# Foreign rows of the recurrence gates gathered by DMA, 48 of them stacked as high and low parts

## The chip, the cores and the metric

The kernel runs on one core of one Trainium2 chip. The metric is the device time in microseconds of one execution. The time of a kernel is the median over several executions.

## The reference

Two layers over 256 tokens with a width of 1024. Each layer norms x, projects it in one wide product, and feeds two branches. Branch A is an attention with 8 heads whose keys an indexer has chosen. Branch B is a recurrence of width 1408: a causal convolution of four taps, then two gates r and i, a scan over positions, and an output product. Both branches are gated, added, projected and added to x. A last norm ends the computation.

The change touches only the gates of branch B:

```
xb = x.reshape(B, S, RNN_BLOCKS, RNN_BLOCK_DIM)       # 16 blocks of 88 channels
r = sigmoid(einsum('bsnc,ncd->bsnd', xb, w_r) + b_r)  # each block has its own 88x88 matrix
i = sigmoid(einsum('bsnc,ncd->bsnd', xb, w_i) + b_i)
```

A gate channel depends on the 88 convolved channels of its own block alone. All products keep nearly the precision of float32.

## The kernel before

**Layout.** Channels lie on partitions, tokens along the free dimension. The 1408 channels of branch B are 11 tiles of 128 (`KR`). Blocks of 88 do not line up with tiles of 128, so the blocks that a tile of outputs touches reach into one or both neighbour tiles. These rows of a neighbour are called foreign here. The block matrices are laid out on the host as one block-diagonal 1408x1408 matrix, and a gate multiplies 128x128 cuts of it.

**Precision.** Every operand is split into a high part (rounded to the matmul's type, `copy`) and a low part (the rest, `sub`). A product takes three matmuls, high weight by high data, low weight by high data and high weight by low data (`mm3`, L617); the matmuls are recorded under L493, the line of the helper `mm`. A data tile `xs` is `[128, 2, 256]`: high and low halves of 256 tokens.

**Gates.** `gate_parts` (L96) lists what a gate of tile j multiplies. Odd tiles below 10 have foreign rows on both sides that fit in half a tile each; for these `gr` (L944) copies half of a neighbour's `xs` into a shared tile `xm` (two copies for each mixed tile, 10 in a layer), and the gate multiplies the tile itself and `xm`. The other tiles multiply whole neighbour tiles, whose weights are mostly zeros. Tiles 2, 4, 6 and 8 need three tiles, all others two. Each of the two gates r and i needs three matmuls of 256 columns for each tile: 12 in a gate with two tiles, 18 in one with three, 156 in a layer.

**The weight stream.** All weights are cut on the host into 128x128 blocks in the order in which the plan uses them (`weight_stream`, L1188; `unit_blocks`, L108) and loaded as chunks of 8 blocks, 512 KB, by SP's DMA queue (SPq). A chunk lands in one of 4 `raw` buffers (`RAWS`), ScalarE or VectorE rounds it to `wh`, VectorE subtracts to get `wl`; both have 6 buffers (`WBUF`). All DMAs of the kernel are issued by SP.

**Order.** `plan` (L62) writes out the units of a layer: the indexer; then for j = 0..10 the recurrence input `xr` and its gate `gr` (24 matmuls each) with light units of other projections between them, and `gate` of tile j-3 behind `gr` of tile j (`DELAY`); after the last `gr` the gates of tiles 8, 9 and 10, each behind two light units; then attention and the outputs. Every operation is first entered in a list. `Program.issue` (L266) then simulates the engines with costs written in the code and fixes the order of instructions on each engine, SP's DMAs included; the engines carry it out in that order and wait on semaphores for their data. TensorE's order follows the position in the plan. An operation that makes a new tile needs a free buffer of its pool: `r2` has 38 (`xs`, `xm` and others), `f1` has 21 of 1 KB per partition (convolution outputs `xc`, gate `sg`, `y`, `asq`, scan results `hh`, and others). `choose` (L375) lets an operation take a buffer ahead of earlier ones only while enough stay free for those (up to 5 in `f1`, `KEEP`, L406). After gates 2, 5, 8 and 10 a `tail` of three (at last two) tiles runs the exponentials, the scan into `hh` and the products.

Of the kernel before, what the change touches and what calls it, by code (L numbers as in the profile page):

```python
# [11 lines left out]
F32 = mybir.dt.float32  # L12
F32R = mybir.dt.float32r
# [4 lines left out]
P = 128  # L18
D = 1024
T = 256  # L20
# [3 lines left out]
KR = NR // P  # L24
NH = 8
NB = 16
BD = NR // NB
# [19 lines left out]
NPAR = _c  # L47


def gate_rows(j):  # L50

    lo = (P * j) // BD * BD
    hi = ((P * j + P - 1) // BD + 1) * BD
    return list(range(lo // P, (hi - 1) // P + 1))


DELAY = 3
# [38 lines left out]
def gate_parts(j):  # L96


    rows = gate_rows(j)
    if len(rows) == 3:  # L100
        first = (P * j) // BD * BD
        last = ((P * j + P - 1) // BD + 1) * BD
        if P * j - first <= 64 and last - P * (j + 1) <= 64:
            return [j, (j + 1, j - 1)]
    return rows


def unit_blocks(u):  # L108

    n = u[0]  # L110
    if n == "ik":
        return [("in80", k, OFF["ik"]) for k in range(KD)]
    if n == "attn":
        return []
    if n in ("iq", "ga", "xr", "gr", "q", "k"):
        return [("in", k, OFF[n] + u[1] * P) for k in range(KD)]
    if n == "gate":
        return [(w, i, u[1] * P) for w in ("rg", "ig") for i in gate_parts(u[1])]
    if n in ("v", "mb", "ma"):
        return [("in", 2 * u[2] + k, OFF[n] + u[1] * 512 + a * P) for k in range(2) for a in range(4)]  # L120
    if n == "yb":
        return [("or", k, u[1] * 512 + a * P) for k in range(KR) for a in range(4)]
    if n == "ya":
        return [("oa", k, u[1] * 512 + a * P) for k in range(KD) for a in range(4)]
    return [("o", k, u[1] * P) for k in range(u[2], u[3])]
# [64 lines left out]
def real(a):  # L190
    return a.ap() if isinstance(a, V) else a
# [222 lines left out]
def trunk(ctx, tc, xT, pos, par, wst, out):  # L414
    nc = tc.nc
# [3 lines left out]
    fp = ctx.enter_context(tc.tile_pool(name="fp", bufs=1))  # L419
    pp = ctx.enter_context(tc.tile_pool(name="pp", bufs=1, space=bass.MemoryType.PSUM))  # L420
    ctx.enter_context(tc.manual_schedule())
    pg = Program()
    cnt = [0]

    def nm(s):
        cnt[0] += 1
        return f"{s}{cnt[0]}"


    def const(s, shape, dt=F32, bufs=1, tag=None):  # L430
        return pg.tile(cp, tag or s, [P] + shape, dt, nm(s), bufs)

    def r2(s):
        return pg.tile(rp, "r2", [P, 2, T], F32R, nm(s), R2)
# [7 lines left out]
    def f1(s):  # L442
        return pg.tile(fp, "f1", [P, T], F32, nm(s), F1)

# [4 lines left out]
    def act(o, i, func, **kw):  # L449
        c = (50 if i.psum() else 94) + 0.833 * o.size() + (200 if "accum_out" in kw else 0)  # L450
        aps = [kw[k] for k in ("scale", "bias") if isinstance(kw.get(k), V)]
        outs = [o] + ([kw["accum_out"]] if "accum_out" in kw else [])
        pg.op("act", c + 93 * len(aps), outs, [i] + aps,
              lambda: nc.scalar.activation(real(o), real(i), func, **{k: real(v) for k, v in kw.items()}),
              TABS.get(func))

    def copy(o, i):

        n = o.size()
        pg.op("act", (50 if i.psum() else 94) + 0.833 * n, [o], [i],  # L460
              lambda: nc.scalar.activation(real(o), real(i), AF.Copy),  # L461
              alt=(67 + 1.046 * n if i.psum() else 69 + 0.52 * n,
                   lambda: nc.vector.tensor_copy(real(o), real(i))))
# [5 lines left out]
    def mul(o, a, b):  # L469
        tt(OP.mult, o, a, b)  # L470
# [20 lines left out]
    def mm(o, w, m, start, stop, grp=False, cost=None):  # L491
        pg.op("pe", cost or (m.size() + 32) / 2.4, [o], [w, m],
              lambda: nc.tensor.matmul(real(o), real(w), real(m), start=start, stop=stop, skip_group_check=grp))  # L493
# [14 lines left out]
    class Stream:  # L508
        def __init__(self):
            self.pos = 0  # L510
            self.raws = {}
            self.parts = {}
            self.nload = 0
# [65 lines left out]
    ws = Stream()  # L579
# [4 lines left out]
    first = ws.load(QUARTERS)  # L584
# [13 lines left out]
    def pc(n, i=0):  # L598
        return prm[:, PC[n] + i:PC[n] + i + 1]
# [17 lines left out]
    def mm3(o, rhs, first, last, grp=False):  # L617
        wh, wl = ws.block()
        mm(o, wh, rhs[0], first, False, grp)
        mm(o, wl, rhs[0], False, False, grp)  # L620
        mm(o, wh, rhs[1], False, last, grp)

    def proj(o, rhs):
        n = len(rhs)
        for k in range(n):
            mm3(o, rhs[k], k == 0, k == n - 1)

    def split(dst, src):

        copy(dst[0], src)  # L630
        sub(dst[1], src, dst[0].bitcast(F32))

    def halves(t):
        return t[:, 0, :], t[:, 1, :]
# [148 lines left out]
    class Layer:  # L783
        def __init__(self, l, xg, norm):
            self.l = l
            self.xg = xg
            self.norm = norm
            self.h = []
            self.sga, self.sma, self.smb = {}, {}, {}
            self.xc, self.xs, self.rix, self.sy, self.g = {}, {}, {}, {}, {}  # L790
            self.rope = {}
            self.mix = {}
            self.aT = []
            self.m = []
            self.banks = {}
            self.wk = [const("wk0", [P]), const("wk1", [T])]
            self.kh = const("kh", [T], F32R)
            self.kl = const("kl", [T], F32R)
            self.iwq = const("iwq", [2, 16])
# [144 lines left out]
        def gr(self, j):  # L944
            ps = self.banks["rnn"]
            proj(ps[:, 1, :], self.h)
            n = KR * self.l + j
            c = f1("xc")
            w = [pc("cw", 4 * n + i) for i in range(4)]
            act(c, ps[:, 0, :], AF.Identity, scale=w[3], bias=pc("cb", n))  # L950
            for i in (2, 1, 0):
                s = 3 - i
                stt(c[:, s:], ps[:, 0, :T - s], w[i], c[:, s:], OP.mult, OP.add)
            t = r2("xs")
            split(halves(t), c)
            self.xc[j], self.xs[j] = c, halves(t)
            for i, h in ((j - 1, slice(0, 64)), (j + 1, slice(64, 128))):
                if 0 <= i < KR and any(isinstance(r, tuple) for r in gate_parts(i)):
                    if i not in self.mix:
                        self.mix[i] = r2("xm")  # L960
                        self.xs[i + 1, i - 1] = halves(self.mix[i])
                    copy(self.mix[i][h], t.bitcast(F32)[h])
            u = f1("sg")
            act(u, ps[:, 1, :], AF.Sigmoid)
            mul(u, u, ps[:, 1, :])
            self.sy[j] = u

        def gate(self, j):
            rows = gate_parts(j)
            ps = bank("pq", "gps")  # L970
            for gi in range(2):
                for n, i in enumerate(rows):
                    mm3(ps[:, gi, :], self.xs[i], n == 0, n == len(rows) - 1)
            n = KR * self.l + j
            t = r2f("rix")
            r, ix, y = t[:, 0, :], t[:, 1, :], f1("y")
            act(r, ps[:, 0, :], AF.Sigmoid, bias=pc("br", n))
            act(ix, ps[:, 1, :], AF.Sigmoid, bias=pc("bi", n))
            mul(ix, ix, self.xc[j])
            act(y, r, AF.Tanh, scale=cpos[:, n:n + 1])  # L980
            self.rix[j] = (t, y)
            if j in GROUPS:
                self.tail(GROUPS[j])
# [175 lines left out]
    n = 0  # L1159
    for w in (1, 2, 2, 2, 1):  # L1160
        o = f2("fo")[:, :w, :]
# [10 lines left out]
QUARTERS = 2  # L1172
R2 = 38
F2 = 5
F1 = 21
RAWS = 4
WBUF = 6
LEAD = 2000.0
# [9 lines left out]
def weight_stream(w_in, w_rg, w_ig, w_oa, w_or, w_o):  # L1188

    out = []  # L1190
    for l in range(L):
        mats = {"in": w_in[l], "or": w_or[l], "oa": w_oa[l], "o": w_o[l]}
        mats["in80"] = w_in[l].copy()
        mats["in80"][:, OFF["ik"] + 80:] = 0
        for n, w in (("rg", w_rg[l]), ("ig", w_ig[l])):
            d = np.zeros((NR, NR), w.dtype)
            for b in range(NB):
                d[b * BD:b * BD + BD, b * BD:b * BD + BD] = w[b]
            mats[n] = d
        for u in plan():  # L1200
            for n, r, c in unit_blocks(u):
                if isinstance(r, tuple):
                    lo, up = r[0] * P, r[1] * P + 64
                    out.append(np.concatenate([mats[n][lo:lo + 64, c:c + P], mats[n][up:up + 64, c:c + P]]))
                else:
                    out.append(mats[n][r * P:r * P + P, c:c + P])
    assert len(out) == NBLK
    out += [np.zeros((P, P), w_in.dtype)] * (NCH * 8 - NBLK)
    a = np.stack(out).reshape(NCH, 8, P, P)
    return np.ascontiguousarray(a.transpose(0, 2, 1, 3)).reshape(NCH, P, 1024)  # L1210
# [45 lines left out]
```

## Time and profile before

| | |
|---|---|
| median of 3 executions | 716.36 us (716.25, 716.36, 757.32) |
| the profiled execution | 716.78 us, of which the span is 715.0 us |
| TensorE matmuls (PE) | 699.0 us busy, 4880 of them |
| VectorE (DVE) | 599.8 us busy |
| ScalarE (ACT) | 499.2 us busy |
| GpSimd (POOL) | 7.7 us busy |
| DMA, queue of SP | 120.44 MB, 51.3% of 16 engines' span |
| granted TensorE clock | 0.995 of 2.4 GHz |

PE rows are matmuls, PEld rows are weight loads, which overlap them. A matmul's recorded duration (283 ns) overlaps with that of the next, so the pace of a run of matmuls is read from the length of the run divided by its count. SPq rows are DMAs as SP issues them. `L493` is the one line that records nearly every matmul, so matmuls are told apart by the names of their tiles: `rps` (xr and gr), `gps` (the gates), `ga`, `ma`, `mb` (light units), `yb`, `ya`, `ops` (outputs).

### The profile page before, as it was taken

To read this page: it belongs to the slowest core of one execution; us is meant where nothing else is said; L and a number is where in the kernel's file an instruction comes from. 1 tells how busy PE (TensorE), PEld (TensorE's weight loads), DVE (VectorE), ACT (ScalarE), POOL (GpSimd) and SP (SyncE) were. 2 spreads that over 40 slices of the span, in tenths; PEclk is the share of its full clock that TensorE was granted. 3 is DMA by queue.
4 is the path that set the end of the run, shared out by engine and by line. 5 is a ranking of instruction groups with operands and counts; after the bars stand their busy time and mean duration, and the time that the engine had idled before them with its cause. 6 is when DMAs were issued, how large, how long until landed. Compare 5 with 4: busy or idle time off the path is not lost.

```text
span 715.0 us, 12814 instructions
## 1 busy us (share of the span) xinstructions
PE 699.0 (98%) x4880; PEld 652.5 (91%) x4880; DVE 599.8 (84%) x1181; ACT 499.2 (70%) x811; POOL 7.7 (1%) x18
## 2 busy tenths in 40 slices
PE   7999999999999999999999999999999999999996
PEld 6998999999999998888999899999999898988895
DVE  6989999899798959857779998989889886896652
ACT  7997685899895648434669776698879674764432
POOL 0000000000000000000000000010000000000000
PEclk9999999999999999999999999999999999999998
DMA  7646455555656452655553554555555545445501
GB/s 255 207 160 215 159 171 181 179 177 189 198 173 207 148 179 86 203 180 178 177 177 116 182 175 166 184 182 181 179 202 180 199 152 177 148 130 180 191 1 60
DMA packets 35485, 121.26 MB, mean 170 GB/s; under 512 B 3936, under 2 KB 6496, under 8 KB 35424
## 3 DMA queue, kind: packets, MB, share of 16 engines
q1 hardware_dynamic: 35424, 120.44, 51.3%
q8 instruction: 38, 0.62, 0.3%
q14 instruction: 23, 0.19, 0.1%
HBM read 119.38 MB, written 1.05 MB: 168 GB/s over the span
## 4 chain that ended last, share of the span: by engine, by line
PE 86%; ACT 6%; DVE 3%; issue 1%; DMA 1%; SPq 1%; DVEq 0%; ACTq 0%
PE rps L493 16%; PE yb L493 8%; PE ops L493 7%; PE k L493 6%; PE q L493 6%; PE ma L493 6%; PE v L493 6%; PE ya L493 6%; PE gps L493 5%; PE ga L493 5%; PE mb L493 5%; ACT wh L461 3%; PE dots L493 2%; PE lg L493 2%; PE av L493 2%
## 5 line engine op out<-in xcount | busy, mean ns | idle before, releaser
L467 DVE TENSOR_TENSOR wl<-raw,wh 128x1024 fp32r<-128x1024 f32 x223 | 271.6, 1220 | 67.3 <-ACT wh L461 66.2
L461 ACT ACTIVATE wh<-raw 128x1024 fp32r<-128x1024 f32 x199 | 210.4, 1058 | 134.3 <-PE ya L493 22.9
L493 PE MATMUL rps<-hl,wh 128*128 128x256 f32 x352 | 99.6, 283 | 0.0
L493 PE MATMUL rps<-hh,wl 128*128 128x256 f32 x352 | 99.6, 283 | 0.0
L493 PE MATMUL rps<-hh,wh 128*128 128x256 f32 x352 | 99.6, 283 | 0.0
L493 PEld LDWEIGHTS rps<-hh,wh 128*128 128x128 f32 x352 | 67.5, 192 | 0.2
L493 PEld LDWEIGHTS rps<-hh,wl 128*128 128x128 f32 x352 | 67.5, 192 | 0.2
L493 PEld LDWEIGHTS rps<-hl,wh 128*128 128x128 f32 x352 | 67.5, 192 | 0.0
L493 PE MATMUL yb<-wh,g 128*128 128x512 f32 x176 | 58.9, 396 | 0.0
L493 PE MATMUL iq<-xg,wh 128*128 128x256 f32 x240 | 44.7, 284 | 0.0
L493 PE MATMUL ya<-wh,aT 128*128 128x512 f32 x128 | 40.3, 393 | 0.0
L493 PEld LDWEIGHTS iq<-xg,wh 128*128 128x128 f32 x240 | 37.9, 192 | 0.0
L493 PEld LDWEIGHTS yb<-wh,g 128*128 128x128 f32 x176 | 32.5, 188 | 5.3
L493 PE MATMUL ga<-hl,wh 128*128 128x256 f32 x128 | 36.3, 284 | 0.7 <-DVE hl L467 0.7
L493 PE MATMUL ops<-ml,wh 128*128 128x256 f32 x128 | 36.8, 287 | 0.0
L493 PE MATMUL ops<-mh,wl 128*128 128x256 f32 x128 | 36.7, 287 | 0.0
L493 PE MATMUL ops<-mh,wh 128*128 128x256 f32 x128 | 36.6, 286 | 0.0
L493 PE MATMUL q<-hh,wl 128*128 128x256 f32 x128 | 36.4, 284 | 0.0
L493 PE MATMUL q<-hh,wh 128*128 128x256 f32 x128 | 36.3, 284 | 0.0
L493 PE MATMUL k<-hh,wl 128*128 128x256 f32 x128 | 36.3, 284 | 0.0
L493 PE MATMUL q<-hl,wh 128*128 128x256 f32 x128 | 36.2, 283 | 0.0
L493 PE MATMUL ga<-hh,wl 128*128 128x256 f32 x128 | 36.2, 283 | 0.0
(230 smaller groups left out, 1998.4 us busy)
## 6 DMA issues: line engine op xcount, KB each, us to landing
raw<-in_wst_dram SPq DMA_DIRECT2D x223, 512.0 KB, 3.4
raq<-in_wst_dram SPq DMA_DIRECT2D x8, 128.0 KB, 4.5
x<-in_xT_dram SPq DMA_DIRECT2D x8, 128.0 KB, 3.5
out_dram<-fo SPq DMA_DIRECT2D x3, 256.0 KB, 2.2
out_dram<-fo SPq DMA_DIRECT2D x2, 128.0 KB, 2.1
head<-in_par_dram SPq DMA_DIRECT2D x1, 230.0 KB, 2.6
posi<-in_pos_dram SPq DMA_DIRECT2D x1, 128.0 KB, 3.7
```

The lines of the kernel that those rows point to most:

```text
L461: lambda: nc.scalar.activation(real(o), real(i), AF.Copy),
L467: lambda: nc.vector.tensor_tensor(real(o), real(a), real(b), op=op))
L493: lambda: nc.tensor.matmul(real(o), real(w), real(m), start=start, stop=stop, skip_group_check=grp))
```

## The change

`gate_parts` now lists the foreign rows of a tile exactly (48 for tiles 0, 1, 3, 5, 7, 9 and 10; 136 for tiles 2, 4, 6 and 8). The tile's own product stays three matmuls. Of the foreign rows, 48 are stacked: their high parts lie on partitions 0 to 47 of a tile `xk`, their low parts on partitions 48 to 95, and the weight block holds the 48 weight rows twice. Two matmuls on 96 partitions, with the high and with the low weights, then give all products of these rows (and the product of low by low, which was not there before). The 88 further rows of tiles 2, 4, 6 and 8 go into a tile `xf` on 88 partitions, three matmuls as before.

`xk` (an `f1` buffer, of which there are now 22) and `xf` (an `r2` buffer) are filled by DMAs from the `xs` tiles of the neighbours, from SBUF to SBUF, issued by SP: one DMA for each stretch of rows in one tile and, for `xk`, for each of the two halves. That is 4 DMAs for every gate but the first and the last, which have 2: 40 in a layer, 80 in all. They are one operation in the list, entered with `gate`, with a written cost of 300 ns for each DMA. A row of `xk` is 1 KB, one of `xf` 2 KB. `xm` and its 20 copies go. The count of weight blocks and chunks stays (52 gate blocks in a layer before and after); their contents change.

```diff
--- before.py
+++ after.py
@@ -47,11 +47,14 @@
 NPAR = _c
 
 
-def gate_rows(j):
+def foreign(j):
 
     lo = (P * j) // BD * BD
     hi = ((P * j + P - 1) // BD + 1) * BD
-    return list(range(lo // P, (hi - 1) // P + 1))
+    return list(range(lo, P * j)) + list(range(P * j + P, hi))
+
+
+STACK = 48
 
 
 DELAY = 3
@@ -96,13 +99,21 @@
 def gate_parts(j):
 
 
-    rows = gate_rows(j)
-    if len(rows) == 3:
-        first = (P * j) // BD * BD
-        last = ((P * j + P - 1) // BD + 1) * BD
-        if P * j - first <= 64 and last - P * (j + 1) <= 64:
-            return [j, (j + 1, j - 1)]
-    return rows
+    f = foreign(j)
+    if 2 * len(f) <= P:
+        return [("stack", f)]
+    return [("plain", f[:-STACK]), ("stack", f[-STACK:])]
+
+
+def stretches(rows):
+
+    out = []
+    for n, r in enumerate(rows):
+        if out and out[-1][1] == r // P and out[-1][3] == r % P:
+            out[-1][3] += 1
+        else:
+            out.append([n, r // P, r % P, r % P + 1])
+    return out
 
 
 def unit_blocks(u):
@@ -115,7 +126,11 @@
     if n in ("iq", "ga", "xr", "gr", "q", "k"):
         return [("in", k, OFF[n] + u[1] * P) for k in range(KD)]
     if n == "gate":
-        return [(w, i, u[1] * P) for w in ("rg", "ig") for i in gate_parts(u[1])]
+        out = []
+        for w in ("rg", "ig"):
+            out.append((w, u[1], u[1] * P))
+            out += [(w, tuple(rows * (2 if kind == "stack" else 1)), u[1] * P) for kind, rows in gate_parts(u[1])]
+        return out
     if n in ("v", "mb", "ma"):
         return [("in", 2 * u[2] + k, OFF[n] + u[1] * 512 + a * P) for k in range(2) for a in range(4)]
     if n == "yb":
@@ -789,7 +804,6 @@
             self.sga, self.sma, self.smb = {}, {}, {}
             self.xc, self.xs, self.rix, self.sy, self.g = {}, {}, {}, {}, {}
             self.rope = {}
-            self.mix = {}
             self.aT = []
             self.m = []
             self.banks = {}
@@ -953,24 +967,47 @@
                 stt(c[:, s:], ps[:, 0, :T - s], w[i], c[:, s:], OP.mult, OP.add)
             t = r2("xs")
             split(halves(t), c)
-            self.xc[j], self.xs[j] = c, halves(t)
-            for i, h in ((j - 1, slice(0, 64)), (j + 1, slice(64, 128))):
-                if 0 <= i < KR and any(isinstance(r, tuple) for r in gate_parts(i)):
-                    if i not in self.mix:
-                        self.mix[i] = r2("xm")
-                        self.xs[i + 1, i - 1] = halves(self.mix[i])
-                    copy(self.mix[i][h], t.bitcast(F32)[h])
+            self.xc[j], self.xs[j] = c, t
             u = f1("sg")
             act(u, ps[:, 1, :], AF.Sigmoid)
             mul(u, u, ps[:, 1, :])
             self.sy[j] = u
 
+        def gather(self, kind, rows):
+
+            parts = stretches(rows)
+            src = {i: self.xs[i] for _, i, _, _ in parts}
+            moves = []
+            if kind == "plain":
+                dst = r2("xf")
+                for d, i, a, z in parts:
+                    moves.append((dst[d:d + z - a], src[i][a:z]))
+            else:
+                dst = pg.tile(fp, "f1", [P, T], F32R, nm("xk"), F1)
+                for h in range(2):
+                    for d, i, a, z in parts:
+                        d += h * len(rows)
+                        moves.append((dst[d:d + z - a], src[i][a:z, h, :]))
+            pg.op("dma", 300 * len(moves), [dst], list(src.values()),
+                  lambda: [nc.sync.dma_start(real(o.bitcast(F32)), real(i.bitcast(F32))) for o, i in moves][-1])
+            return dst
+
         def gate(self, j):
-            rows = gate_parts(j)
+            parts = [(kind, len(rows), self.gather(kind, rows)) for kind, rows in gate_parts(j)]
             ps = bank("pq", "gps")
             for gi in range(2):
-                for n, i in enumerate(rows):
-                    mm3(ps[:, gi, :], self.xs[i], n == 0, n == len(rows) - 1)
+                o = ps[:, gi, :]
+                mm3(o, halves(self.xs[j]), True, False)
+                for n, (kind, k, m) in enumerate(parts):
+                    last = n == len(parts) - 1
+                    wh, wl = ws.block()
+                    if kind == "plain":
+                        mm(o, wh[:k], m[:k, 0, :], False, False)
+                        mm(o, wl[:k], m[:k, 0, :], False, False)
+                        mm(o, wh[:k], m[:k, 1, :], False, last)
+                    else:
+                        mm(o, wh[:2 * k], m[:2 * k], False, False)
+                        mm(o, wl[:2 * k], m[:2 * k], False, last)
             n = KR * self.l + j
             t = r2f("rix")
             r, ix, y = t[:, 0, :], t[:, 1, :], f1("y")
@@ -1172,7 +1209,7 @@
 QUARTERS = 2
 R2 = 38
 F2 = 5
-F1 = 21
+F1 = 22
 RAWS = 4
 WBUF = 6
 LEAD = 2000.0
@@ -1200,8 +1237,9 @@
         for u in plan():
             for n, r, c in unit_blocks(u):
                 if isinstance(r, tuple):
-                    lo, up = r[0] * P, r[1] * P + 64
-                    out.append(np.concatenate([mats[n][lo:lo + 64, c:c + P], mats[n][up:up + 64, c:c + P]]))
+                    m = np.zeros((P, P), w_in.dtype)
+                    m[:len(r)] = mats[n][list(r), c:c + P]
+                    out.append(m)
                 else:
                     out.append(mats[n][r * P:r * P + P, c:c + P])
     assert len(out) == NBLK
```

## Rows read from the trace of the kernel before

**Rows 1.** The page: busy us (share of the span) and instructions of each engine.
```profile
PE 699.0 (98%) x4880; PEld 652.5 (91%) x4880; DVE 599.8 (84%) x1181; ACT 499.2 (70%) x811; POOL 7.7 (1%) x18
```

**Rows 2.** Stretches: us, busy us (x instructions) by engine, PEclk, DMA share, GB/s.
```profile
0.00:18.00 18.00, 12.88 (x68) 11.09 (x69) 11.38 (x32) 13.15 (x29) 1.28 (x10) 1.00 0.78 253
...
98.00:210.00 112.00, 112.00 (x826) 107.00 (x825) 103.26 (x221) 93.89 (x157) 2.47 (x4) 1.00 0.57 184
...
110.00:122.00 12.00, 12.00 (x91) 11.51 (x90) 12.00 (x38) 6.89 (x11) 0.00 (x0) 1.00 0.56 190
...
460.00:548.00 88.00, 88.00 (x645) 83.92 (x645) 78.75 (x145) 74.78 (x124) 3.17 (x2) 1.00 0.57 186
...
640.00:715.00 75.00, 67.98 (x424) 60.97 (x422) 40.12 (x59) 27.91 (x41) 0.00 (x0) 0.96 0.34 111
```

**Rows 3.** Waits of TensorE: us in total, times, longest; the longest of nine.
```profile
PE nps L493 <- DVE nsq L724: 3.8, 1, 3.8
```

**Rows 4.** The page: the chain that ended last, by line.
```profile
PE rps L493 16%; PE yb L493 8%; PE ops L493 7%; PE k L493 6%; PE q L493 6%; PE ma L493 6%; PE v L493 6%; PE ya L493 6%; PE gps L493 5%; PE ga L493 5%; PE mb L493 5%; ACT wh L461 3%; PE dots L493 2%; PE lg L493 2%; PE av L493 2%
```

**Rows 5.** Chain in time: start us, us, what; around late gates of either layer.
```profile
181.41 2.16 PE gps L493 x18
183.57 2.88 PE ga L493 x24
...
189.19 1.43 PE gps L493 x12
...
533.66 1.43 PE gps L493 x12
```

**Rows 6.** Groups by line: the gates' matmuls, and one group of their loads.
```profile
L493 PE MATMUL gps<-xs,wh 128*128 128x256 f32 x168 | 35.6, 284 | 0.0
...
L493 PEld LDWEIGHTS gps<-xs,wh 128*128 128x128 f32 x168 | 28.4, 191 | 0.7
...
L493 PE MATMUL gps<-xs,wl 128*128 128x256 f32 x84 | 23.7, 283 | 0.0
...
L493 PE MATMUL gps<-xm,wh 128*128 128x256 f32 x40 | 10.5, 283 | 0.0
...
L493 PE MATMUL gps<-xm,wl 128*128 128x256 f32 x20 | 5.7, 283 | 0.0
```

**Rows 7.** Tile xm: ns min/median/max, first and last start us, of its copies.
```profile
L461 ACT ACTIVATE xm<-xs x17: 615/627/632, 81.3 to 521.3; 64x512 fp32r<-64x512 f32 x17
L463 DVE CAST xm<-xs x3: 415/420/425, 129.5 to 497.7; 64x512 fp32r<-64x512 f32 x3
```

**Rows 8.** SP in time: start us, us, two issues one behind the other.
```profile
5.91 0.43 SPq L499 DMA_DIRECT2D raq<-in_wst_dram  x1
6.38 0.43 SPq L499 DMA_DIRECT2D x<-in_xT_dram  x1
```

**Rows 9.** Waits of SP from 98 to 210 us; first and last of 12.
```profile
SPq L499 <- DVE wl L467: 39.3, 16, 3.8
...
SPq L499 <- DVE y L486: 2.5, 1, 2.5
```

**Rows 10.** Waits of ScalarE from 98 to 210 us: the longest on TensorE.
```profile
ACT wh L461 <- PE rps L493: 3.5, 3, 1.7
```

**Rows 11.** DMA from 98 to 210 us: queue, raw; whole span: raq, out.
```profile
q1 hardware_dynamic: 5606, 20.44, 56.3%
...
raw<-in_wst_dram SPq DMA_DIRECT2D x38, 512.0 KB, 3.4
...
raq<-in_wst_dram SPq DMA_DIRECT2D x8, 128.0 KB, 4.5
...
out_dram<-fo SPq DMA_DIRECT2D x2, 128.0 KB, 2.1
```

**Rows 12.** VectorE in time: the last xs, the last hh of a tail.
```profile
176.96 0.42 DVE L467 TENSOR_TENSOR xs<-xc,xs 128x256 fp32r<-128x256 f32 x1
...
202.19 0.68 DVE L1007 TENSOR_TENSOR_SCAN hh<-rix 128x256 f32<-128x256 f32 x1
```

## The prediction, made before the changed kernel was run

> **What bounds the kernel now.** I read the busy shares first. TensorE's matmuls cover 699.0 of 715.0 us, VectorE follows with 599.8 [rows 1]. A share can hide stages, so I took stretches next: in both recurrence stages, from 98 to 210 us and from 460 to 548 us, the matmuls fill the stretch to the last hundredth, with PEclk 1.00; the 16.0 us that TensorE is not busy lie mostly in the first 18 us (18.00 - 12.88 = 5.1) and the last 75 (75.00 - 67.98 = 7.0) [rows 2]. The waits of TensorE agree: the longest of nine is at the norm's sums, and none is at a gate [rows 3]. The chain that ended last is almost only matmuls, 5% of it `gps`, the gates [rows 4]. So time in these stages is the count of matmuls times their pace, as long as nothing else becomes late.
>
> The pace is not the 283 ns of a record, since records overlap. From the chain in time, 18 gate matmuls take 2.16 us and 24 of `ga` 2.88 us: 0.120 us each at 256 columns; the 12 of a gate with two tiles take 1.43 [rows 5].
>
> **What is removed.** The gates now have 168 + 84 + 40 + 20 = 312 matmuls [rows 6], which is 2 x 156. After the change a gate with 48 foreign rows has 2 x (3 + 2) = 10 in place of 12, one with 136 has 2 x (3 + 3 + 2) = 16 in place of 18. Every gate loses 2, whatever its kind: 22 gates x 2 = 44 matmuls, 44 x 0.120 = **5.28 us** [rows 5]. They lie on the path, for TensorE has no idle time there.
>
> The copies into `xm` go too: 17 x 0.627 = 10.7 us of ScalarE and 3 x 0.420 = 1.3 us of VectorE [rows 7]. I cost this at nothing: neither engine is waited for at the gates, and no start-up or tail work is among it.
>
> **What is added on TensorE.** 136 of the remaining 268 matmuls have fewer rows: 22 gates x 2 x 2 on 96 partitions and 8 x 2 x 3 on 88. The trace has none with fewer than 128 rows. One bound: the price goes with the rows, then 88 x 0.120 x 32/128 + 48 x 0.120 x 40/128 = 2.6 + 1.8 = 4.4 us more are gained. The other: the load of such a block, 191 ns recorded [rows 6], is no longer hidden beside the matmul before it, then 136 x 0.191 = 26.0 us are lost. I take nothing: the nearest rows, full gates and `ga`, have different operands and one pace, set by 256 columns that stay.
>
> By the Trainium skill, TensorE: Matmul & The Clock Gate, section LDWEIGHTS, a load's time goes by its columns and not by its rows; no run here shows that yet, and by it the sum stays as it is. Against the change speaks TensorEngine Tiling (Array Packing) in the same skill, Key Properties: changing the tiling mode drains TensorE. Its list has modes of 128, 64 and 32 rows; if 88 or 96 rows counted as a change of mode, that would be the drain rival below; the list has no such mode, so I give it little.
>
> **What is added on SP.** 80 DMAs. Two issues in a row stand 6.38 - 5.91 = 0.47 us apart [rows 8], so 80 x 0.47 = 37.6 us of SP's time, 18.8 in each layer, and at most 4 x 0.47 = 1.9 us at one gather. In the 112 us from 98 to 210 SP waits 100.9 us, 12 entries from 39.3 down to 2.5, nearly all for VectorE to free `raw` buffers [rows 9]. There is room; the cover is SP's idle time. Behind a gather on SP stand the weight loads. A gather waits for the neighbour's `xs`, whose last instruction is VectorE's subtraction; the `raw` buffers that the loads behind it need are freed by VectorE too, later in its fixed order, so this wait mostly takes the place of one already there. If a load is late by 1.9 us, the cover is the weights already converted: ScalarE's conversions wait for TensorE to free `wh` buffers [rows 10], so up to five further chunks of 8 blocks lie ready, 5 x 24 x 0.120 = 14.4 us. Cost: nothing.
>
> **What is added on the DMA engines.** A layer's gathers write 11 x 96 x 1 KB + 4 x 88 x 2 KB = 1.76 MB, beside 20.44 MB of the stretch at a share of 56.3% [rows 11]; in proportion about 61%. No cost.
>
> **The new wait.** The first foreign matmul of a gate waits for the gather, and all of TensorE's queue stands behind it. From issue to landing takes between 2.1 us (`out`) and 4.5 us (`raq`) [rows 11]; I take 4.5 for a cautious sum: behind a weight load just issued (3.4), four issues and the landing make 3.4 + 1.9 + 4.5 = 9.8 us after `xs`. The tightest gate is that of tile 9, which needs the `xs` of tile 10, the last: ready at 176.96 + 0.42 = 177.38 [rows 12]; the gate's matmuls begin at 189.19, and in the second layer at 533.66 [rows 5]. That leaves 11.8 us, so even the slow sum arrives. The other gates follow their last `xs` by more, since a whole pair of `xr` and `gr` (48 x 0.120 = 5.8 us) and light units lie between. Cost: nothing, bounds 0 and what the first rival gives.
>
> **Sum.** The profiled execution took 716.78 us, the span and 1.78 around it. 716.78 - 5.28 = 711.50. The median of the runs is 0.42 below the profiled execution, so the forecast for the median is 716.36 - 5.28 = **711.1 us**, 0.7% less. A comparison of this kernel can tell about 2% (14.3 us) from no change, so the verdict would be no change.
>
> **Rival 1, late gathers.** An `xk` needs an `f1` buffer, and the written order gives it one ahead of earlier tiles only while up to 5 stay free. The gather of gate 9 is entered behind the tail of tiles 6 to 8, whose last `hh` is made at 202.19 [rows 12]. If the pool were that tight, the gather would land at about 202.87 + 1.9 + 4.5 = 209.3, 20.1 us after the gate's turn. TensorE can go on with later units, but their weights sit behind the gate's, and 14.4 us of them are ready: up to 5.7 us of stall, twice 11.4, and the time is up to 722.5. The small end is one late gather of 1 us, 712. For it: one buffer more, while two or three `xk` live at a time; the 20.1 us. Against it: what lives there by the code (five `sg`, three `xc`, three `y`) leaves about half of the 21 buffers free, and lead times are 11.8 us and more. Price 712 to 722.5, middle 716. The skill's DMA: Bandwidth & Descriptors, Rules for kernel authors, wants small transfers joined, for below 64 KB they are mostly overhead; here that overhead would be this lateness, and the trace's landings do not yet show it for pieces of 8 to 96 KB.
>
> **Rival 2, drained loads (slower).** The place is each of the 136 matmuls with 88 or 96 rows; the price at most one unhidden load of 191 ns. It decides from 5.28 / 136 = 39 ns each (no gain left) and makes the verdict slower from (5.28 + 14.3) / 136 = 144 ns. At the whole price: 711.1 + 26.0 = 737.1. For it: no row shows such a matmul. Against it: loads of 191 ns run at a pace of 120 ns already, beside the matmul before them, also where the operands change from `ga` to `gps` [rows 5].
>
> **Rival 3, the gain comes back as another wait.** The conversion of weights could be the true pace: VectorE is busy 12.00 of 12.00 us from 110 to 122 us, while the choice of keys runs [rows 2]. Then TensorE would only wait where it worked before, and the time is 716. Against it: ScalarE waits for TensorE in the same stage [rows 10], and both engines get 12 us less to do. That the change does not do what it says is not open: 312 matmuls become 268 by the lists of blocks; if some padding kept them, the time would be 716 as well.
>
> **How the numbers follow.** Forecast 0.76; rival 1 0.14; rival 2 0.04; rival 3 0.06. The range takes in the gain by rows (711.1 - 4.4 = 706.7) and rival 1 to beyond its middle: 707 to 718; left out are rival 2, the upper part of rival 1 and a new order of instructions at start and end that costs more than the gain. Faster by 2% (below 702) needs more than any bound gives: 0.01. Slower by 2% (above 730.7) is rival 2 and a heap of late gathers: 0.05. The rest, 0.94, is no change.
>
> **What would show it.** Right: 4836 matmuls; `gps` with 268 at a pace of 0.120 us, runs of 10 and 16 taking 1.2 and 1.9 us; PE busy about 693.7; no wait of TensorE for a DMA of `xk` or `xf`; the waits of ScalarE for TensorE still there; a share of DMA some 5 points higher in the stage. Rival 1: rows of PE waiting for `xk<-xs`, in gates 9, 3 or 6. Rival 2: gaps beside loads of 88 or 96 rows in an unbroken run. Rival 3: PE waiting for `wl` or `wh` in the recurrence stages. The forecast is wrong if the idle time of TensorE there is no longer zero.

## The result, and the profile after

The changed kernel took 711.83 us (median of 4, 711.33 to 712.05), the kernel before 716.73 beside it; the ratio is 0.9933 with a 95% interval from 0.9913 to 0.9952. One of the four executions of the kernel before ran in a slower state (757.32 us) and is left out of the ratio, by which the gain is 4.8 us. The forecast was 711.1, its range 707 to 718. Timed again in a later session it took 711.31 (710.88 to 711.55), ratio 0.9922 [0.9909, 0.9935], a gain of 5.6 us. By the 2% bound this is no change; by its own interval the kernel is 0.5 to 0.9% faster.

The page of the profiled execution, with the lines that answer to [rows 1]:

```profile
span 709.6 us, 12900 instructions
## 1 busy us (share of the span) xinstructions
PE 693.7 (98%) x4836; PEld 647.9 (91%) x4836; DVE 598.0 (84%) x1178; ACT 488.8 (69%) x794; POOL 6.4 (1%) x18
```

The span fell by 715.0 - 709.6 = 5.4 us, the busy time of TensorE by 699.0 - 693.7 = 5.3; 44 matmuls are gone. What it is not busy stayed, 16.0 before and 15.9 after. The stretches that answer to [rows 2]:

```profile
0.00:18.00 18.00, 13.67 (x68) 11.84 (x69) 11.15 (x32) 12.76 (x29) 1.29 (x10) 1.00 0.76 253
...
98.00:210.00 112.00, 112.00 (x821) 106.77 (x820) 104.84 (x224) 94.35 (x155) 2.49 (x4) 1.00 0.62 200
...
460.00:548.00 88.00, 88.00 (x649) 84.08 (x648) 81.12 (x144) 71.94 (x121) 0.83 (x2) 1.00 0.64 205
```

TensorE is still without a gap in both recurrence stages, and the share of the DMA engines rose from 0.57 to 0.62. The longest wait of TensorE is the one at the norm's sums, as in [rows 3], and its waits hold neither `xk` nor `xf`:

```profile
PE nps L508 <- DVE nsq L739: 3.9, 1, 3.9
```

The chain in time shows runs of 16 and 10 in place of the 18 and 12 of [rows 5]:

```profile
179.25 1.92 PE gps L508 x16
181.17 2.88 PE ga L508 x24
...
186.79 1.19 PE gps L508 x10
```

1.92 / 16 = 0.120 us, 1.19 / 10 = 0.119: the pace is that of full matmuls. The loads and matmuls on 96 and 88 rows, from the view of the tile `gps` (ns min/median/max, first and last start in us):

```profile
L508 PEld LDWEIGHTS gps<-xk,wh x44: 187/192/192, 98.8 to 535.8; 96*128 96x128 f32 x44
L508 PE MATMUL gps<-xk,wh x44: 281/283/284, 98.9 to 535.9; 96*128 96x256 f32 x44
...
L508 PEld LDWEIGHTS gps<-xf,wh x32: 192/192/192, 115.8 to 522.2; 88*128 88x128 f32 x32
L508 PE MATMUL gps<-xf,wh x32: 283/283/283, 115.9 to 522.3; 88*128 88x256 f32 x32
```

They have the durations of the 128-row ones. Now the gather that has the least time, that of gate 9: VectorE's last instruction of its source, SP's first and last issue, then the time from issue to landing. The profile records that time for few DMAs: in this stage only for 48 KB ones issued between 164 and 168 us, for none of gate 9's own.

```profile
175.25 0.42 DVE L482 TENSOR_TENSOR xs<-xc,xs 128x256 fp32r<-128x256 f32 x1
```
```profile
175.74 0.69 SPq L992 DMA_DIRECT2D xk<-xs  x1
...
178.08 0.73 SPq L992 DMA_DIRECT2D xk<-xs  x1
```
```profile
DMA to landing us min/median/max: 4.2/4.2/4.2
```

The rows are ready at 175.67, the last DMA is issued from 178.08 and has landed, by an estimate with that 4.2, at about 178.08 + 4.2 = 182.3. The first foreign matmul of the gate comes after three of its own tile, at 186.79 + 0.36 = 187.15. So about 4.9 us of lead were left (the lead of a gather is the time by which it lands before its first matmul).

In the same 112 us SP waits 34.9 us at most for one cause, and 84.3 us in all over 22 entries (100.9 us in [rows 9]):

```profile
SPq L514 <- DVE wl L482: 34.9, 15, 3.5
```

### The profile page after: what moved, and what is told of

It reads as the page before. It is cut to its first block, busy times and chain, and to the rows that moved or that the text cites. A ratio compares the mean times of both kernels' runs of the same rounds, so it can differ in the third digit from the quotient of the medians.

```text
span 709.6 us, 12900 instructions
## 1 busy us (share of the span) xinstructions
PE 693.7 (98%) x4836; PEld 647.9 (91%) x4836; DVE 598.0 (84%) x1178; ACT 488.8 (69%) x794; POOL 6.4 (1%) x18
## 4 chain that ended last, share of the span: by engine, by line
PE 82%; DVE 8%; ACT 6%; issue 2%; DMA 1%; SPq 0%; DVEq 0%; ACTq 0%
PE rps L508 15%; PE yb L508 9%; PE ops L508 7%; PE k L508 6%; PE q L508 6%; PE ma L508 6%; PE v L508 6%; PE ya L508 6%; PE gps L508 5%; PE mb L508 4%; PE ga L508 4%; DVE wl L482 2%; ACT wh L476 2%; PE lg L508 2%; PE av L508 2%
## 5 line engine op out<-in xcount | busy, mean ns | idle before, releaser
L508 PE MATMUL k<-hh,wh 128*128 128x256 f32 x128 | 36.2, 283 | 0.0
```

## The experiments

**Theory**: the gain is 44 matmuls at 0.120 us, and everything that was added is hidden. **Rivals**: the gain is the copies' or the new order's; the gathers cost something by SP, by the DMA engines or by lateness; short matmuls cost something.

**One matmul more in each stack.**

```diff
                     else:
+                        mm(o, wh[:2 * k], m[:2 * k], False, False)
                         mm(o, wh[:2 * k], m[:2 * k], False, False)
                         mm(o, wl[:2 * k], m[:2 * k], False, last)
```

> The changed kernel with the first matmul of every stack (96 rows, high weights) done twice: 44 matmuls more, so the count is again 4880; everything else, the gathers too, stays. The stacked rows are counted double in the result. Theory (the gain is the count of matmuls times 0.120 us): 711.8 + 5.3 = 717.1 us, ratio to the kernel before 1.000 to 1.002, and runs of 12 and 18 gate matmuls again 1.43 and 2.16 us long. Rival (the gain comes from ScalarE's and VectorE's 12 us less of copies, or from the new order): stays at 711.8 to 713, ratio 0.993 to 0.995.

Measured: 717.01 us, ratio 1.0003 [0.9993, 1.0012], forecast 717.1. The page and the chain in time of this kernel:

```profile
PE 699.1 (98%) x4880; PEld 653.3 (91%) x4880; DVE 598.1 (84%) x1178; ACT 489.2 (68%) x793; POOL 8.8 (1%) x18
```
```profile
180.69 2.16 PE gps L508 x18
182.85 2.88 PE ga L508 x24
185.73 2.75 PE ma L508 x12
188.48 1.43 PE gps L508 x12
```

With 4880 matmuls again, the time is that of the kernel before, although the copies are gone, the order is new and the gathers are there. So all of these come to nothing in sum, within the 0.9 us of the interval, and the count is the gain. The copies' 12 us of ScalarE and VectorE can only have brought something if the gathers or the order cost as much; the next kernel takes the gathers out of that sum.

**No gathers.**

```diff
-            parts = [(kind, len(rows), self.gather(kind, rows)) for kind, rows in gate_parts(j)]
+            parts = [(kind, len(rows), self.xs[j] if kind == "plain" else self.xs[j][:, 0, :]) for kind, rows in gate_parts(j)]
```

> The changed kernel without its 80 gather DMAs: the matmuls on 96 and 88 rows read the tile's own rows in place of the gathered ones (so the foreign rows' products are left out), count and order of matmuls stay. Theory (gathers are hidden in SP's idle time, and no gate waits for one): 711.8, within 0.7 of the changed kernel, ratio 0.993. Rival (the gathers cost something that the trace does not show as a wait of TensorE, by SP, by the DMA engines or by the f1 buffers): 709 to 710.5.

Measured: 711.75 us, ratio 0.9929 [0.9917, 0.9942]; the span is 709.6, as with gathers. 80 DMAs, 3.5 MB and the waits for them cost nothing that can be measured, at this place and in this number. (Without the gathers the written order of the other engines comes out a little different: ScalarE has 789 instructions in place of 794, VectorE 1182 in place of 1178.)

**Further copies of the DMAs of a stack: one, then three.** They go into columns of a tile that is dead by then. The written cost stays that of the real DMAs (`real_moves`), so that the order of instructions stays too and does not make room for them.

```diff
+            real_moves, outs = len(moves), [dst]
+            if kind == "stack":
+                outs.append(posi)
+                sh = posi.bitcast(F32)
+                for s in range(1):          # 3 in the second kernel
+                    q = slice(64 * s, 64 * s + 64)
+                    moves = [(sh[d + h * len(rows):d + h * len(rows) + z - a, q], src[i][a:z, h, q])
+                             for h in range(2) for d, i, a, z in parts] + moves
-            pg.op("dma", 300 * len(moves), [dst], list(src.values()),
+            pg.op("dma", 300 * real_moves, outs, list(src.values()),
```

> The changed kernel with each DMA of a stack issued twice, the further copy first, with a quarter of the columns, into a tile that nobody reads: 64 DMAs more on SP, the gathers of a gate land about 4 x 0.77 = 3.1 us later. In the changed kernel the gather of gate 9 lands at about 182.3 us and is wanted at 187.1 (4.8 us of lead), all other gates have more. Theory (lateness counts only beyond the lead): 711.8, ratio 0.993, no wait of TensorE for xk. Rival (SP's time is the cost, weight loads come late): 713 or more, waits of ScalarE for raw grow.

> The same with three further copies ahead of each DMA of a stack: 192 DMAs more on SP, the gathers of a gate land about 12 x 0.77 = 9.2 us later, which is 4.4 us beyond the lead of gate 9. Theory: TensorE waits for xk at gate 9 of both layers, about 4 us each, time 716 to 721, all of the loss in these two waits. Rival A (the lead is longer than I read it): 711.8 to 712.5. Rival B (SP becomes the bound: 96 further issues in a layer, some 74 us beside about 90 us of idle time in the stage, delay the weight loads): TensorE waits for wl or wh at many places, 722 or more.

Measured: 710.38 us (ratio 0.9914 [0.9901, 0.9928]) with one copy, 753.68 (1.0514 [1.0496, 1.0532]) with three. One copy costs nothing. Three cost 42 us, where the theory gave 4 to 9, and rival B named the cause. Here are the waits of SP from 98 to 210 us, the longest of either kernel, first with one copy (20 entries, 64.3 us in all), then with three (17 entries, 24.8):

```profile
SPq L514 <- DVE wl L482: 23.5, 12, 3.5
```
```profile
SPq L1000 <- DMA raw<-in_wst_dram: 4.7, 5, 1.4
```

Over the four kernels SP's spare time falls from 100.9 to 84.3, 64.3 and 24.8 us: it runs short only in the last. There SP issues almost without a pause. One gather with its copies takes 12.4 us, and the weight loads stand behind it:

```profile
136.20 9.30 SPq L1000 DMA_DIRECT2D posi<-xs  x12
145.61 3.00 SPq L1000 DMA_DIRECT2D xk<-xs  x4
148.71 8.33 SPq L514 DMA_DIRECT2D raw<-in_wst_dram  x6
```

The waits of that kernel show the way on to TensorE:

```profile
ACT wh L476 <- DMA raw<-in_wst_dram: 70.5, 26, 9.9
DVE wh L478 <- DMA raw<-in_wst_dram: 30.5, 7, 8.5
...
PE gps L508 <- DMA xk<-xs: 18.6, 4, 7.4
...
PE ma L508 <- DVE ga L482: 6.5, 2, 6.1
```

The conversions wait for weights, and behind them, in the fixed order of ScalarE and VectorE, stand the convolutions whose `xs` the next gather needs. So the lateness of one gather can make the next one late, which is read from that order and was not tested apart. The chain that ended last, shares by engine on the page of this kernel, runs for 10% over DMAs and for 5% over SP's issues; in the changed kernel these have 1% and 0%:

```profile
PE 52%; DVE 19%; DMA 10%; ACT 9%; SPq 5%; issue 4%; DVEq 0%; ACTq 0%
```

TensorE's time that is not busy grows from 15.9 to 750.9 - 707.7 = 43.2 us, and its busy time by 14.0, for the granted clock is 0.92 of 2.4 GHz in the stage from 98 to 210 us, a mean of its two levels of 1.2 and 2.4 GHz. The longest record of a matmul on `xk`, the first behind a wait of TensorE, is 554 ns in place of 283:

```profile
L508 PE MATMUL gps<-xk,wh x44: 282/283/554, 99.0 to 576.4; 96*128 96x256 f32 x44
```

Rival B is confirmed in its cause; the waits of TensorE for `wl` or `wh` that it named are small (0.9 and 0.6 us), while those for the gathered rows are 18.6 us.

**Matmuls on 64 rows.**

```diff
-                        mm(o, wh[:2 * k], m[:2 * k], False, False)
-                        mm(o, wl[:2 * k], m[:2 * k], False, last)
+                        mm(o, wh[:64], m[:64], False, False)
+                        mm(o, wl[:64], m[:64], False, last)
```

> The changed kernel with the matmuls of the stacks on 64 rows in place of 96 (the last 32 of the stacked rows are left out of the products); gathers and counts stay. It puts a price on short matmuls at a row count that is a tiling mode of its own in the Trainium skill's TensorEngine Tiling (Array Packing). Theory (the pace goes by columns): 711.8, ratio 0.993, runs of 10 and 16 gate matmuls 1.19 and 1.92 us long as with 96 rows. Rival (a change of row mode drains TensorE: in and out of the mode twice in each of 22 gates, 88 changes, each up to one unhidden load of 0.19 us): up to 711.8 + 16.8 = 728.6, with gaps of about 0.1 to 0.2 us beside the matmuls on 64 rows.

Measured: 728.29 us, ratio 1.0167 [1.015, 1.0184]. The theory fell, the rival's upper end of 728.6 was met. Starts of TensorE's matmuls (us), from the last light unit into a gate:

```profile
106.27 0.28 PE L508 MATMUL gps<-xs,wh 128*128 128x256 f32 x1
106.48 0.38 PE L508 MATMUL gps<-xk,wh 64*128 64x256 f32 x1
106.70 0.28 PE L508 MATMUL gps<-xk,wl 64*128 64x256 f32 x1
106.91 0.38 PE L508 MATMUL gps<-xs,wh 128*128 128x256 f32 x1
107.13 0.28 PE L508 MATMUL gps<-xs,wl 128*128 128x256 f32 x1
107.25 0.28 PE L508 MATMUL gps<-xs,wh 128*128 128x256 f32 x1
```

And the loads at the first change:

```profile
106.16 0.19 PEld L508 LDWEIGHTS gps<-xs,wh 128*128 128x128 f32 x1
106.48 0.18 PEld L508 LDWEIGHTS gps<-xk,wh 64*128 64x128 f32 x1
```

At a change of row count two steps are long, 0.21 and 0.22 in place of 0.12, about 0.19 us for each change; the load at the change begins with its own matmul and not one matmul earlier. 88 changes x 0.19 = 16.7, beside 728.29 - 711.83 = 16.5 measured. The changed kernel steps evenly by 0.12 at its changes between 128, 88 and 96 rows:

```profile
161.92 0.28 PE L508 MATMUL gps<-xs,wh 128*128 128x256 f32 x1
162.04 0.28 PE L508 MATMUL gps<-xf,wh 88*128 88x256 f32 x1
...
162.28 0.28 PE L508 MATMUL gps<-xf,wh 88*128 88x256 f32 x1
162.40 0.28 PE L508 MATMUL gps<-xk,wh 96*128 96x256 f32 x1
162.52 0.28 PE L508 MATMUL gps<-xk,wl 96*128 96x256 f32 x1
162.64 0.28 PE L508 MATMUL gps<-xs,wh 128*128 128x256 f32 x1
```

The Trainium skill says in TensorEngine Tiling (Array Packing), Key Properties, that changing the tiling mode drains TensorE. The 0.19 us at each change between 128 and 64 rows agree with it. The even steps show that 88 and 96 rows cost no such change here.

**The buffer and the lead.**

```diff
-F1 = 22
+F1 = 21
```

> The changed kernel with 21 f1 buffers, as before the change, in place of 22. Theory (the pool has room, rival 1 of the prediction has no ground): 711.8 within 0.7, TensorE waits for no gather. Rival (the 22nd buffer is what keeps the gathers early): 713 to 718, waits of TensorE for xk after a tail.

Measured: 711.15 us, ratio 0.9928 [0.9913, 0.9942], no wait of TensorE for a gather. The 22nd buffer is not needed for the time; the order of TensorE's instructions was the same with 21.

```diff
-DELAY = 3
+DELAY = 1
```

> The changed kernel with every gate planned one tile behind its xr and gr in place of three (DELAY 1): the neighbour's rows are made and gathered (about 3.1 us of issues and 4.2 to landing) shortly before the gate wants them. Theory (a late gather costs only what the units behind it and the converted weights, some 14 us, don't cover): between 711 and 716, waits of TensorE for xk, if any, of a few us in all. Rival (the gathers need the lead of three tiles, 22 gates late by about 3 to 7 us each): 750 or more.

> The kernel before with the same DELAY 1, to compare the last with: there the foreign rows come by copies of 0.63 us. Theory: 716 to 718, so the changed kernel keeps at least 1 us and at most 5.3 of its gain at this lead. Rival (the gathers need the lead): 716 to 718 here, and a changed kernel that is slower than it.

Measured: 726.57 us for the changed kernel (ratio 1.0157 [1.0112, 1.0201]), 718.78 for the one before (1.003 [1.002, 1.004], forecast 716 to 718). Both numbers that I gave for the changed kernel missed, 711 to 716 and 750 or more, but of the two the rival has the sign: at this lead the change loses 7.8 us where it won 4.8. A wait of that kernel, and its place in the chain:

```profile
PE gps L508 <- DMA xf<-xs: 9.7, 5, 3.9
...
PE gps L508 <- DMA xk<-xs: 1.1, 1, 1.1
```
```profile
175.78 4.55 DMA xf<-xs
180.33 0.14 issue
180.47 0.59 PE gps L508 x3
```

10.8 us of waits lie at a few gates. TensorE's time that is not busy is 726.0 - 699.4 = 26.6 us, 10.7 more than in the changed kernel, and its busy time is 5.7 longer, with a granted clock of 0.97 and 0.98 in the stretches of the two stages that stand in [rows 2], again behind waits. Nothing covers a late gather, since TensorE's order is fixed: the converted weights lie ready (ScalarE's conversions wait 15.3 us for the matmuls on `xk`, 3.9 in the changed kernel), but the matmuls that would use them stand behind the waiting one. That the order places the gate too early fits its written costs (300 ns for an issue, 2.0 us to landing, where the trace has some 0.77 and 4.2 us); a kernel with other costs was not run.

**The changed kernel and the one with one copy, side by side.**

> The changed kernel itself once more, beside the next one. It was 711.8 when it was first timed. Theory (the 710.4 of the kernel with one shadow copy is within what two programs with the same order on TensorE, ScalarE and VectorE differ by from session to session): 710.5 to 712, the next one within 0.7 of it. Rival (the further DMAs make it faster): 711.8 here and 710.4 there again.

> The kernel with one further copy of each DMA of a stack once more, on the same chip as the last one. Theory: within 0.7 of the changed kernel beside it. Rival: 1.4 us faster than it, as before; then the place is to be read from the stretches of TensorE's idle time, at the start and at the seam between the layers.

Measured: 711.31 (710.88 to 711.55) and 710.45 (710.16 to 711.34). They differ by 0.9 us, a little more than the theory allowed and less than the rival; the intervals of their ratios, [0.9909, 0.9935] and [0.9894, 0.9925], overlap. Whether the further DMAs bring some tenths stays open; none of these variants beats the changed kernel clearly.

## Why the prediction was right

- **The bound and the sum.** Count times pace in an unbroken stretch of TensorE: 44 x 0.120 = 5.28. Measured 5.3 of busy time, 5.4 of span, 4.8 by the ratio and 5.6 by that of the later session; the doubled matmuls of the first experiment gave it all back.
- **Copies at nothing.** Right within the interval: the copies stayed away in that experiment, the time was the old one, and the gathers by themselves cost nothing.
- **Short matmuls at nothing.** Right for 96 and 88 rows, and neither bound was touched. The reason given was too wide: that 256 columns set the pace whatever the rows fails at 64 rows, where a change costs 0.19 us. Rival 2 got 0.04. What it describes, a load that is no longer hidden, does happen here, though not at 88 or 96 rows; its price of 0.191 us is what a change to or from 64 rows costs. Stacks of 64 rows, as in that experiment, made the kernel slower than the one before. That the stacks have 96 rows and not 64 decided the sign, and no row of the kernel before could tell.
- **SP at nothing.** Right in the result, the size was off: 4 issues took 178.08 + 0.73 - 175.74 = 3.07 us, 0.77 each and not the 0.47 of [rows 8]; in the timeline the gathers of the two layers take 29.7 + 28.4 = 58.1 us of SP and not 37.6. The spare time of [rows 9] was enough; it lasts for one further copy and not for three (two were not tried).
- **The DMA engines.** Forecast 61%, measured 0.62 in the stage. That they agree so well is partly luck: the forecast put all 1.76 MB of a layer's gathers into these 112 us, where 1.3 MB of them lie, and the stretch of the changed kernel holds one weight load of 0.5 MB more (39 in place of 38). The pieces are 8 to 160 KB, not 8 to 96.
- **The new wait.** The cautious sum was 9.8 us after `xs`; it took about 182.3 - 175.67 = 6.6. Its first term, 3.4 us behind a weight load just issued, did not come: SP had issued one at 175.36, and began the gather at 175.74, not after that load had landed. Its second, the issues, was too small (3.07 in place of 1.9). From `xs` to the first foreign matmul there were 187.15 - 175.67 = 11.5 us, of which about 4.9 were left, so no gate waited.
- **Rival 1.** Its condition, a tight `f1` pool, was not met with 21 or 22 buffers. Its working held a mistake that the lead of one tile shows: it lets TensorE go on with later units, against what the prediction says itself under the new wait, that all of TensorE's queue stands behind the first foreign matmul. With the lead of one tile TensorE stood still for 10.8 us in all, with converted weights ready. The 14.4 us of converted weights can cover late weight loads, not late data.
- **Rival 3.** Excluded: no time came back as a wait of TensorE in the recurrence stages, and ScalarE's conversions still waited for TensorE to free buffers. Their entry for the recurrence inputs, over the whole span (18.8 us in the kernel before):

```profile
ACT wh L476 <- PE rps L508: 19.9, 19, 1.8
```

## What to carry to other kernels

Where one engine is busy without a gap, a change is worth its instructions times their pace in a run. What it adds elsewhere is free as long as each queue it joins has spare time and each datum arrives before its turn. Both can be read as margins (here 84 of 112 us of SP's waits, 4.9 us of lead). A margin is not elastic: in a fixed order a late datum stops the engine for all its lateness, and a full issue queue can make the next data late in turn. Packing few rows into matmuls paid here at 88 and 96 rows and lost at 64; measure the step between starts on both sides of such a matmul.

## What the runs showed of the hardware

- Matmuls on 88 and 96 rows with 256 columns run at 0.120 us like those on 128. On 64 rows each change between 64 and 128 rows costs about 0.19 us, split over the two steps at the change. Between 64 and 88 rows nothing was tried.
- A small SBUF to SBUF DMA took SP 0.59 us (median; 0.50 to 1.33), about 0.77 from start to start in the gather of gate 9. Its landing took 3.2 to 4.2 us where the profile records it, for pieces of 48 KB; a 512 KB weight load took 3.5.
- With 18.6 us of waits for gathered rows (three further copies) the granted clock from 98 to 210 us was 0.92 of 2.4 GHz on average, with 10.8 us (lead of one tile) 0.97 there and 0.98 in the other recurrence stage; in the changed kernel, without such waits, it was 1.00 in both.
